# Value and HGRN-gate columns of w_in by seven half-size products (Strassen), with the gate's silu kept in DRAM

## The chip, the cores and the metric

One NeuronCore of a Trainium2 chip runs the whole kernel. Its engines work side by side, each through its own list of instructions in order: TensorE (PE: matmuls, with its weight loads PEld), VectorE (DVE), ScalarE (ACT), GpSimd (POOL) and SyncE (SP), which here mostly issues DMAs. They wait for one another by semaphores. The metric is the device time of one execution in microseconds; three runs were taken, and one more with the profiler.

## The reference, cut to what matters

```python
u = rmsnorm(h, g_pre)                  # 1024 tokens x 2048, float32
z = u @ w_in                           # w_in: 2048 x 9216
aq, ak, av, ag, hq, hf_f, hf_b, hv, hg = jnp.split(z, SPLIT_IDX, axis=-1)   # 1024 columns each
...
o_fw = hgrn2_direction(qh, vh, heads(hf_f, HG_HEADS), lb_f)    # scan over the tokens, 8 heads of 128
...
o_hg = rmsnorm(o_fw + o_bw, g_hg).reshape(B, S, HG_W)
y_hg = o_hg * jax.nn.silu(hg.astype(f32))
y = jnp.concatenate([y_att, y_hg], axis=-1) @ w_out
```

The columns of `w_in` that matter here are av (2048 to 3071), hv (7168 to 8191) and hg (8192 to 9215). Behind this follow the output product, two normalizations and a gated embedding product, which the change doesn't touch.

## The kernel before

float32 products are made of three matmuls each: both operands are split into a rounded high part and a residual, and high x high, high x residual and residual (bfloat16) x high are added up in one PSUM bank. `K.uh` holds the high part of the normalized activations u, transposed (two halves of 512 tokens, 16 tiles of 128 rows of K each), `K.ul` their residual in bfloat16. A weight piece (`piece`, line 71) is loaded into `raw` (three buffers), rounded by ScalarE (`wh`, line 82), its residual taken by GpSimd, now and then by VectorE (`wl`, line 83), and cast to bfloat16 by VectorE (`wb`, line 84). `wh`, `wl` and `wb` have three buffers each.

The program has these stages. First x is normalized in eight tiles of 128 tokens (`prenorm`): ScalarE squares, VectorE scales (line 167), TensorE transposes (line 171), ScalarE and VectorE split the result into `uh` (line 150) and `ul` (line 151). Beside it and after it `v_group` makes the 2048 value columns in four groups of 512, with a bank for each 128 tokens and 16 steps of K; a step has 24 matmuls for 8 banks. The group's first two quarters of the tokens stand between the tiles of the normalization. The results go to `vD` in DRAM.

Then comes the HGRN loop, eight heads (`hgrn`). A head has four column groups of 128 columns (`group`, 96 matmuls of 512 columns each): forget gate forward and backward (into `F2`), query (`hq`), and gate (`hgt`, by `gate_evac`, which multiplies with the sigmoid). Between them stands the scan: a ladder of seven levels in which VectorE multiplies prefix products (line 281, tiles `X`, `O`, `Q2`, `TB`), with small matmuls on each level (`pl`, `pa`, lines 275, 300 and 307); then transposes (`ptr`), state products (`pu`, line 366) with a chain of VectorE additions (`hst`, line 372), output products (`pout`, lines 385 to 389), the normalization over a head (`hsq`, `hss`, `hon`, line 398), and, after the next head's first group (`flush`, `finish`), transposes (`po`) and the product with `hgt` (`hyt`, line 407). After that come eight attention units and the output stages.

PSUM has eight banks: four of the name `gb` for column groups, four for all else (`wk`: `xp`, `vb`, `pl`, `pa`, `ptr`, `pu`, `pout`, `po`). A scheduler that knows the program order, buffers and priorities sets each engine's list; weight pieces of the groups are given a higher priority, so they are fetched early. Inside the list of an engine nothing overtakes.

Of the kernel before, what the change touches and what calls it, by code (L numbers as in the profile page):

```python
# [21 lines left out]
S = 1024  # L22
D = 2048
INW = 9216
KT = 16
# [3 lines left out]
NGB = 4  # L29
# [7 lines left out]
def f32(t):  # L37
    return t.bitcast(F32)
# [6 lines left out]
class Kern:  # L45
    def __init__(self, tc, ctx):
        self.tc = tc
        self.nc = tc.nc
        self.ctx = ctx
        nc = self.nc  # L50
        self.cp = ctx.enter_context(tc.tile_pool(name="cp", bufs=1))
        self.wp = ctx.enter_context(tc.tile_pool(name="wp", bufs=3))
        self.ps = ctx.enter_context(tc.tile_pool(name="ps", bufs=1, space=PSUM))
        self.dr = ctx.enter_context(tc.tile_pool(name="dr", bufs=1, space=DRAM))
        self.ident = self.cp.tile([128, 128], F32, name="ident")
        make_identity(nc, self.ident)
        self.rest = None
# [170 lines left out]
    def hgrn(self, w_in, h, vsrc, yout):  # L228
        nc = self.nc
        V = nc.vector  # L230
# [13 lines left out]
        base = 4096 + 128 * h  # L244
# [3 lines left out]
        q = big.tile([128, S], F32, name="hq", tag="hq", bufs=1)  # L248
# [7 lines left out]
        TB = big.tile([128, 2032], F32, name="TB", tag="ht", bufs=1)  # L256
# [9 lines left out]
        n = S  # L266
# [15 lines left out]
        while B < 128:  # L282
# [29 lines left out]
            x = X[:, :]  # L312
# [23 lines left out]
            n = nb  # L336
# [22 lines left out]
        for d in range(2):  # L359
# [3 lines left out]
            for g in (order[:4], order[4:]):  # L363
                p = self.wk("pu", (128, 4, 128))
# [341 lines left out]
def tile_hybrid(ctx, tc, x, p, positions, w_in, w_out, g_pre, g_post, g_hg, lb_fwd, lb_bwd, w_pg, w_pp, g_ple, out):  # L706
    nc = tc.nc
    K = Kern(tc, ctx)
    x2 = x[0]
    out2 = out[0]  # L710
    w_in = w_in[0]
# [14 lines left out]
    V = nc.vector  # L726
    vD = [K.dr.tile([S, 512], F32, name=f"vD{i}") for i in range(4)]

    def v_group(cg, toks, pool):
        c0 = (2048, 2560, 7168, 7680)[cg]  # L730
        pb = {t: (K.gb() if t < NGB else K.wk("vb")) for t in toks}
        for k in range(KT):
            wh, wl, wb = K.piece(w_in[128 * k:128 * k + 128, c0:c0 + 512], [512], prio=False,
                                 sub=V if len(toks) == 2 and k % 2 else None)
            for t in toks:
                hi = K.uh[t // 4][:, k, 128 * (t % 4):128 * (t % 4) + 128]
                nc.tensor.matmul(pb[t], hi, wh, start=(k == 0), stop=False)  # L737
                nc.tensor.matmul(pb[t], hi, wl, start=False, stop=False)  # L738
            for t in toks:
                lo = K.ul[t // 4][:, k, 128 * (t % 4):128 * (t % 4) + 128]  # L740
                nc.tensor.matmul(pb[t], lo, wb, start=False, stop=(k == KT - 1))
        for t in toks:
            vo = pool.tile([128, 512], F32, name="vo", tag="vo", bufs=3)
            (nc.scalar.copy if t % 2 else V.tensor_copy)(vo, pb[t])
            nc.sync.dma_start(vD[cg][128 * t:128 * t + 128, :], vo)

    with tc.tile_pool(name="p0", bufs=1) as p0:
        warm = K.sp.tile([128, 1], F32, name="warm", bufs=1)
        V.memset(warm, 1.0)
        nc.scalar.activation(warm, warm, AF.Sqrt)  # L750
        K.prenorm(x2, g_pre, p0, (0, 1))
        v_group(0, (0, 1), p0)
        K.prenorm(x2, g_pre, p0, (2, 3))
        v_group(0, (2, 3), p0)
        late = K.prenorm(x2, g_pre, p0, (4, 5, 6, 7))
        v_group(0, (4, 5, 6, 7), p0)
        with tc.issue_after(late[0].ins), tc.issue_after(late[1].ins):
            K.hg_consts((lb_fwd, lb_bwd), g_hg)
# [269 lines left out]
```

## Time and profile before

| | us |
|---|---|
| median of three runs (2910.19 to 2912.11) | 2910.5 |
| the profiled execution | 2911.69 |
| its span, first to last instruction | 2909.9 |
| TensorE busy | 2785.7 |
| VectorE busy | 1508.4 |
| GpSimd busy | 1023.8 |
| ScalarE busy | 925.5 |

The mean granted TensorE clock was 0.992 of full speed. A row of a group gives line, engine, operation, output <- inputs, shape and count, then the busy time and the mean duration of one. A row of the timeline gives start and duration in us, then the same names; in brackets stands how long the engine had been idle and what ended that. Busy times of matmuls overlap, so the pace of matmuls is read from their starts, not from their durations.

### The profile page before, as it was taken

To read this page: it belongs to the slowest core of one execution; us is meant where nothing else is said; L and a number is where in the kernel's file an instruction comes from. 1 tells how busy PE (TensorE), PEld (TensorE's weight loads), DVE (VectorE), ACT (ScalarE), POOL (GpSimd) and SP (SyncE) were. 2 spreads that over 40 slices of the span, in tenths; PEclk is the share of its full clock that TensorE was granted. 3 is DMA by queue.
4 is the path that set the end of the run, shared out by engine and by line. 5 is a ranking of instruction groups with operands and counts; after the bars stand their busy time and mean duration, and the time that the engine had idled before them with its cause. 6 is when DMAs were issued, how large, how long until landed. Compare 5 with 4: busy or idle time off the path is not lost. (4 is left out here: it accounts for less than half of the span.)

```text
span 2909.9 us, 46582 instructions
## 1 busy us (share of the span) xinstructions
PE 2785.7 (96%) x18128; PEld 1885.7 (65%) x18384; DVE 1508.4 (52%) x2833; ACT 925.5 (32%) x1672; POOL 1023.8 (35%) x769
## 2 busy tenths in 40 slices
PE   6999999999999999999999999999999899999997
PEld 4666666676667676676666666666566566665664
DVE  8601116856346346356655555555755645555555
ACT  5311112222122112124434444443533223333323
POOL 2422223413313313322222222222244554666555
PEclk9999999999999999999999999999999999999998
DMA  6412221211111111121221222122344543433453
GB/s 226 121 55 80 77 86 39 66 52 39 57 52 44 52 52 45 51 65 55 78 70 45 73 76 71 47 74 71 113 122 133 159 142 97 131 113 109 146 155 106
DMA packets 251614, 250.54 MB, mean 86 GB/s; under 512 B 21633, under 2 KB 175233, under 8 KB 250241
## 3 DMA queue, kind: packets, MB, share of 16 engines
q1 hardware_dynamic: 242224, 238.62, 27.6%
q10 hardware_dynamic: 9168, 8.93, 0.9%
q8 instruction: 144, 2.36, 0.3%
q14 instruction: 78, 0.63, 0.1%
HBM read 205.54 MB, written 29.36 MB: 81 GB/s over the span
## 5 line engine op out<-in xcount | busy, mean ns | idle before, releaser
L83 POOL TENSOR_TENSOR wl<-raw,wh 128x512 fp32r<-128x512 f32 x568 | 764.7, 1350 | 1599.8 <-ACT wh L82 1507.1
L84 DVE CAST wb<-raw 128x512 bf16<-128x512 f32 x584 | 430.5, 740 | 785.2 <-PE gb L106 281.8
L82 ACT CAST wh<-raw 128x512 fp32r<-128x512 f32 x584 | 358.4, 617 | 1241.7 <-PE gb L101 414.7
L101 PE MATMUL gb<-uh,wh 128*128 128x512 f32 x1792 | 744.3, 415 | 0.0
L102 PE MATMUL gb<-uh,wl 128*128 128x512 f32 x1792 | 708.6, 395 | 0.0
L106 PE MATMUL gb<-ul,wb 128*128 128x512 bf16 x1632 | 405.7, 380 | 9.8 <-issue 1.8
L101 PEld LDWEIGHTS gb<-uh,wh 128*128 128x128 f32 x1792 | 337.1, 188 | 82.9 <-issue 1.2
L102 PEld LDWEIGHTS gb<-uh,wl 128*128 128x128 f32 x1792 | 337.1, 188 | 68.9 <-issue 1.0
L106 PEld LDWEIGHTS <-wb 128*128 128x128 bf16 x1792 | 158.4, 98 | 204.6 <-issue 54.3
L810 PE MATMUL gb<-wh,yh 128*128 128x512 f32 x512 | 231.2, 452 | 2.8 <-DVE Y L842 2.8
L810 PE MATMUL gb<-wh,th 128*128 128x512 f32 x480 | 215.8, 450 | 0.0
L811 PE MATMUL gb<-wl,yh 128*128 128x512 f32 x512 | 203.7, 398 | 4.7 <-POOL wl L83 4.7
L811 PE MATMUL gb<-wl,th 128*128 128x512 f32 x480 | 190.6, 397 | 5.4 <-POOL wl L83 5.4
L645 DVE CUSTOM_DVE_ANT_1 asm<-asc,amask 128x512 f32<-128x512 f32 x128 | 88.3, 690 | 119.9 <-PE asc L639 119.7
L814 PE MATMUL gb<-wb,yl 128*128 128x512 bf16 x479 | 133.7, 383 | 1.6
L814 PE MATMUL gb<-wb,tl 128*128 128x512 bf16 x452 | 126.2, 384 | 1.0
L650 ACT ACTIVATE asm<-asm,anm 128x512 f32<-128x512 f32 x128 | 92.5, 722 | 90.3 <-DVE anm L648 90.0
L810 PEld LDWEIGHTS gb<-wh,yh 128*128 128x128 f32 x512 | 97.6, 191 | 33.3 <-DVE Y L842 3.3
L737 PE MATMUL gb<-wh,uh 128*128 128x512 f32 x256 | 116.4, 461 | 1.4 <-ACT wh L82 1.3
L811 PEld LDWEIGHTS gb<-wl,yh 128*128 128x128 f32 x512 | 97.4, 190 | 24.3 <-POOL wl L83 5.9
L738 PE MATMUL gb<-wl,uh 128*128 128x512 f32 x256 | 102.4, 407 | 10.9 <-POOL wl L83 7.9
L634 PE MATMUL asc<-ak,aqt 128*32 128x256 bf16 x1536 | 109.7, 401 | 3.2 <-issue 2.4
(274 smaller groups left out, 3668.4 us busy)
## 6 DMA issues: line engine op xcount, KB each, us to landing
raw<-in_w_in_dram SPq DMA_DIRECT2D x320, 256.0 KB
raw<-in_w_out_dram SPq DMA_DIRECT2D x128, 256.0 KB
raw<-in_w_pg_dram SPq DMA_DIRECT2D x128, 256.0 KB
xt<-in_x_dram SPq DMA_DIRECT2D x8, 1024.0 KB
vD<-vo SPq DMA_DIRECT2D x32, 256.0 KB
raw<-yD SPq DMA_DIRECT2D x32, 256.0 KB
xr<-in_x_dram SPq DMA_DIRECT2D x32, 256.0 KB
ak<-ak SPq DMA_DIRECT2D x96, 64.0 KB
```

The costliest lines, as they stand in the source:

```text
L82: nc.scalar.copy(wh, raw)
L83: (sub or nc.gpsimd).tensor_tensor(wl, raw, f32(wh), op=ALU.subtract)
L84: nc.vector.tensor_copy(wb, raw)
L101: nc.tensor.matmul(pb[hf], wh[:, k], self.uh[hf][:, kt], start=(kt == 0), stop=False)
L102: nc.tensor.matmul(pb[hf], wl[:, k], self.uh[hf][:, kt], start=False, stop=False)
L106: mm = nc.tensor.matmul(pb[hf], wb[:, k], self.ul[hf][:, kt], start=False, stop=(kt == KT - 1))
L634: t = nc.tensor.matmul(sc[32 * r:32 * r + 32, :256], qb[:, sq, 32 * r:32 * r + 32], KS[s][:, h, r::4], start=(s == 0), stop=False, skip_gr ...
L737: nc.tensor.matmul(pb[t], hi, wh, start=(k == 0), stop=False)
L738: nc.tensor.matmul(pb[t], hi, wl, start=False, stop=False)
L810: nc.tensor.matmul(pb[t], a, pc[0], start=first, stop=False)
L811: nc.tensor.matmul(pb[t], a, pc[1], start=False, stop=False)
L814: nc.tensor.matmul(pb[t], lo[:, k, 128 * t:128 * t + 128], pc[2], start=False, stop=last)
```

## The change

The value columns (av and hv) and the gate columns (hg) are computed in three blocks of 1024 columns. Each block is a 2 x 2 division of tokens (512 each), K (1024 each) and columns (512 each), and in place of eight half-size products it makes seven, in Winograd's form of Strassen's algorithm: "11", "21", "T2", "T1", "T3", "22" and "T4", each with 8 steps of K and 12 matmuls a step on four banks. Four of them ("T2", "T1", "T3", "22") use sums of the activations. `s_build` makes these four sums once, on VectorE, GpSimd and ScalarE, splits them and writes them to DRAM (`sD`); the blocks read them back through a ring of three buffers (`rh`, `rl`). The weights' differences are made for each block in `weights`, from two or three loaded pieces; `TB` keeps one difference for reuse. Partial results are copied out of PSUM (`copies`) and added. The gate block's results go through sigmoid and product (`z_out`) to `zD` in DRAM, transposed as the loop wants them; the loop loads a head's 128 rows in place of computing the gate group. The normalization is interleaved with product "11" of the first block alone.

```diff
         gt = big.tile([128, S], F32, name="hgt", tag="gt", bufs=1)
-        self.group(w_in, base + 4096, lambda hf, p: self.gate_evac(gt[:, 512 * hf:512 * hf + 512], p))
+        nc.sync.dma_start(gt, self.zD["hg"][h])
...
-    def v_group(cg, toks, pool):
...
+    def s_build(pool, kk):
+        def x(name):
+            return pool.tile([128, 512], F32, name=name, tag=name, bufs=2)
+
+        (a11, l11), (a12, l12), (a21, l21), (a22, l22) = [
+            (f32(K.uh[r][:, kk + 8 * c]), K.ul[r][:, kk + 8 * c]) for r in range(2) for c in range(2)]
+        x0, x1, x2 = x("sx0"), x("sx1"), x("sx2")
+        add(x1, a21, l21, nc.gpsimd)
+        add(x2, a22, l22, nc.gpsimd)
+        add(x0, a11, l11)
+        add(x2, x1, x2)
+        s2 = x("sx3")
+        sub(s2, x2, x0)
+        sub(x1, x0, x1)
+        sub(x0, a12, s2)
+        add(x0, x0, l12)
+        for i, t in enumerate((x2, s2, x1, x0)):
+            h = pool.tile([128, 512], F32R, name="sxh", tag="sxh", bufs=3)
+            l = pool.tile([128, 512], BF16, name="sxl", tag="sxl", bufs=3)
+            nc.scalar.copy(h, t)
+            sub(l, t, f32(h), nc.gpsimd if i == 3 else V)
+            nc.sync.dma_start(sD[i][0][:, kk], f32(h))
+            nc.sync.dma_start(sD[i][1][:, kk], l)
...
+        def raw(self, kk, r, c, second=False):
+            if second:
+                t = ring_pool[0].tile([128, 512], F32, name="rb", tag="rb", bufs=4)
+            else:
+                t = K.wp.tile([128, 512], F32, name="raw", tag="raw", bufs=3)
+            k = kk + 8 * r
+            nc.sync.dma_start(t, w_in[128 * k:128 * k + 128, self.cols[c]:self.cols[c] + 512])
+            return t
...
+            elif name == "T2":
+                t = self.raw(kk, 0, 1)
+                sub(t, t, self.raw(kk, 0, 0, True))
+                d = self.TB[:, kk]
+                sub(d, self.raw(kk, 1, 1, True), t)
+                t = d
+            elif name == "T1":
+                t = self.raw(kk, 1, 1)
+                sub(t, t, self.TB[:, kk])
+            elif name == "T3":
+                t = self.raw(kk, 1, 1)
+                sub(t, t, self.raw(kk, 0, 1, True))
+            else:
+                t = self.raw(kk, 1, 0)
+                sub(t, t, self.TB[:, kk])
...
+            nc.scalar.copy(wh, t)
+            sub(wl, t, f32(wh), nc.gpsimd)
+            V.tensor_copy(wb, t)
...
+            c1 = self.copies(0, "tA")
+            self.open(1)
+            self.product(1, orig(0, 1), "21", True)
+            for c in range(4):
+                add(c1[c], c1[c], self.pb[1][c])
+                self.out(0, 0, c, c1[c])
+            self.TB = ring_pool[0].tile([128, 8, 512], F32, name="TB", tag="TB", bufs=1)
+            self.ring = ring_pool[0]
+            self.product(0, comb(1), "T2", False)
+            u = self.copies(0, "tB")
+            self.open(1)
+            self.product(1, comb(0), "T1", True)
+            p5 = self.copies(1, "tA")
+            self.product(0, comb(2), "T3", False)
+            for c in range(4):
+                add(p5[c], p5[c], self.pb[0][c])
+                self.out(1, 1, c, p5[c])
+            self.product(1, comb(3), "22", False)
+            for c in range(4):
+                add(u[c], u[c], self.pb[1][c])
+                self.out(0, 1, c, u[c])
+            self.product(0, orig(1, 1), "T4", False)
...
+            sg = pool.tile([128, 512], F32, name="zsg", tag="zsg", bufs=2)
+            nc.scalar.activation(sg, t, AF.Sigmoid)
+            nc.gpsimd.tensor_tensor(t, t, sg, op=ALU.mult)
+            nc.sync.dma_start(zD[name][4 * n + c][:, 512 * r:512 * r + 512], t)
...
-        v_group(0, (0, 1), p0)
...
-        for cg in range(1, 4):
-            v_group(cg, tuple(range(8)), p0)
+        b0 = Block((2048, 2560), False, v_out(0), p0, False)
...
+        with tc.tile_pool(name="p0s", bufs=1) as p0s:
+            for kk in range(8):
+                s_build(p0s, kk)
+        with tc.tile_pool(name="p0r", bufs=1) as p0r:
+            ring_pool[0] = p0r
+            b0.run(lambda b: None)
...
+            Block((7168, 7680), False, v_out(2), p0, True).run()
+            Block((8192, 8704), True, z_out("hg", p0), p0, False).run()
```

The line numbers in the pieces that follow are those of the changed kernel: 735 and 738 are the adds and subtractions, 809 the cast `wb`, 761 and 762 the stores of the sums, 779 a weight load, 852 and 853 the loads of the sums, 894 the store of a value tile.

VectorE's list, in the middle of the making of the sums (`sx`: the sums, `sxh` and `sxl` their two parts; `wb_1101` is a piece of product "21"):

```order
L738 TENSOR_TENSOR sxl_810<-sx1_786,sxh_809 128x512
L735 TENSOR_TENSOR sx2_823<-sx1_822,sx2_823 128x512
L809 CAST wb_1101<-raw_1097 128x512
L738 TENSOR_TENSOR sx3_828<-sx2_823,sx0_821 128x512
L738 TENSOR_TENSOR sx1_822<-sx0_821,sx1_822 128x512
L738 TENSOR_TENSOR sxl_834<-sx2_823,sxh_833 128x512
L738 TENSOR_TENSOR sx0_821<-uh0_94,sx3_828 128x512
L738 TENSOR_TENSOR sxl_840<-sx3_828,sxh_839 128x512
L735 TENSOR_TENSOR sx0_821<-sx0_821,ul0_96 128x512
L738 TENSOR_TENSOR sxl_846<-sx1_822,sxh_845 128x512
```

Before, constants and casts of `v_group`'s pieces stood at this place; now 72 such adds stand there, with the casts of product "21" among them, the last cast behind the last add.

SyncE's queue, from the end of the sums to the first loads of product "T2" of the first block (`tA`: the tiles c1):

```order
L761 DMA sh3_108<-sxh_995 128x512
L762 DMA sl3_109<-sxl_996 128x512
L894 DMA vD0_98<-tA_1005 128x512
L894 DMA vD0_98<-tA_1006 128x512
L894 DMA vD0_98<-tA_1007 128x512
L894 DMA vD0_98<-tA_1008 128x512
L852 DMA rh_1186<-sh1_104 128x2048
L853 DMA rl_1187<-sl1_105 128x2048
L779 DMA rb_1192<-in_w_in_dram 128x512
L779 DMA rb_1195<-in_w_in_dram 128x512
```

The loads for "T2" stand behind four stores of results of the products "11" and "21".

TensorE's list in a head of the loop, from the second state products on. Before:

```order
L366 MATMUL pu_3730<-hvt_2955,hk1_3699 128x128 x4
L366 MATMUL pu_3739<-hvt_2955,hk1_3699 128x128 x3
L106 LDWEIGHTS wb_3817
L106 MATMUL gb_3747<-ul0_96,wb_3817 128x512
L106 LDWEIGHTS wb_3817
L106 MATMUL gb_3748<-ul1_97,wb_3817 128x512
```

Now, in the same place of a head:

```order
L366 MATMUL pu_7523<-hvt_6732,hk1_7492 128x128 x4
L366 MATMUL pu_7532<-hvt_6732,hk1_7492 128x128 x3
L385 MATMUL pout_7542<-hvt_6732,ATT_7472 128x128
L106 LDWEIGHTS wb_7665
L106 MATMUL gb_7595<-ul0_96,wb_7665 128x512
L106 LDWEIGHTS wb_7665
L106 MATMUL gb_7595<-ul0_96,wb_7665 128x512
```

`gb_3747` and `gb_3748` are the head's own gate group, `gb_7595` and `gb_7596` the next head's first group (forget gate forward). Before, 29 matmuls of the group follow here, and the products `pout` after them; now 7 follow, then the other `pout`, then 22 matmuls of the group, and then the transposes `po`. In the ladder ahead of this place the next head's group takes the positions of the gate group: 67 matmuls between the same small products.

More of the change, by code (lines that the diff above doesn't have):

```diff
@@ L727, in tile_hybrid @@
     vD = [K.dr.tile([S, 512], F32, name=f"vD{i}") for i in range(4)]
-    def v_group(cg, toks, pool):
[L730 to L745, printed above, removed]
+    sD = [(K.dr.tile([128, 8, 512], F32, name=f"sh{i}"), K.dr.tile([128, 8, 512], BF16, name=f"sl{i}")) for i in range(4)]
@@ new lines, in tile_hybrid, with add, sub @@
+    zD = {n: [K.dr.tile([128, S], F32, name=f"z{n}{i}") for i in range(8)] for n in ("hg",)}
+    def add(out, a, b, eng=None):
+        (eng or V).tensor_tensor(out, a, b, op=ALU.add)
+    def sub(out, a, b, eng=None):
+        (eng or V).tensor_tensor(out, a, b, op=ALU.subtract)
+    def s_build(pool, kk):
[20 more added lines that the diff above has]
+            nc.sync.dma_start(sD[i][1][:, kk], l)
@@ L750, in tile_hybrid, with start @@
         nc.scalar.activation(warm, warm, AF.Sqrt)
-        K.prenorm(x2, g_pre, p0, (0, 1))
-        v_group(0, (0, 1), p0)
[L753 to L758, printed above, removed]
-        for cg in range(1, 4):
-            v_group(cg, tuple(range(8)), p0)
+        b0 = Block((2048, 2560), False, v_out(0), p0, False)
+        late = None
+        with tc.tile_pool(name="p0a", bufs=1) as p0a:
+            def start(b):
+                b.open(0)
+                act = lambda kk: (K.uh[0][:, kk], K.ul[0][:, kk])
+                K.prenorm(x2, g_pre, p0a, (0, 1))
+                b.product(0, act, "11", True, (0, 1))
+                K.prenorm(x2, g_pre, p0a, (2, 3))
+                b.product(0, act, "11", True, (2, 3))
+                return K.prenorm(x2, g_pre, p0a, (4, 5, 6, 7))
+            late = start(b0)
+        with tc.tile_pool(name="p0s", bufs=1) as p0s:
+            for kk in range(8):
+                s_build(p0s, kk)
+        with tc.tile_pool(name="p0r", bufs=1) as p0r:
+            ring_pool[0] = p0r
+            b0.run(lambda b: None)
+            with tc.issue_after(late[0].ins), tc.issue_after(late[1].ins):
+                K.hg_consts((lb_fwd, lb_bwd), g_hg)
+            Block((7168, 7680), False, v_out(2), p0, True).run()
+            Block((8192, 8704), True, z_out("hg", p0), p0, False).run()
+    K.zD = zD
     with tc.tile_pool(name="big", bufs=1) as big:
```

72 lines of the change are left out of this document (added).

## The prediction

> **What bounds the kernel now.** The page's table of busy time comes first, then its strip of 40 slices.
>
> ```profile
> span 2909.9 us, 46582 instructions
> PE 2785.7 (96%) x18128; PEld 1885.7 (65%) x18384; DVE 1508.4 (52%) x2833; ACT 925.5 (32%) x1672; POOL 1023.8 (35%) x769
> PE   6999999999999999999999999999999899999997
> DVE  8601116856346346356655555555755645555555
> ```
>
> TensorE is busy from the second slice to the last, so the kernel is as long as its matmuls, with a weak place only in the first 73 us. So I price matmuls first, and then ask where VectorE (DVE), GpSimd (POOL) or a DMA must finish before TensorE can go on. The stages by the table of windows, and the ends of the stages by the views of lines and sources:
>
> ```profile
> 0.00:100.30 100.30, 71.41 (x322) 46.02 (x328) 80.53 (x142) 55.95 (x95) 33.12 (x28) 0.97 0.60 202
> 100.30:401.40 301.10, 300.21 (x1315) 204.95 (x1337) 51.08 (x134) 47.36 (x78) 80.98 (x64) 1.00 0.26 74
> 655.00:764.10 109.10, 105.26 (x954) 75.60 (x964) 54.52 (x107) 22.34 (x37) 31.94 (x25) 1.00 0.17 49
> 873.00:982.00 109.00, 105.22 (x954) 75.83 (x964) 53.88 (x108) 22.33 (x37) 31.88 (x25) 1.00 0.17 50
> L101 PE MATMUL gb<-uh,wh x1792: 387/389/586, 401.4 to 2047.2; 128*128 128x512 f32 x200
> L407 DVE SCALAR_TENSOR_TENSOR hyt<-po,ghg,hgt x16: 736/740/746, 546.2 to 1309.9; 128x512 f32<-128x512 f32 x16
> ```
>
> The columns after a window's length are PE, weight loads, DVE, ACT, POOL, clock, DMA share and GB/s. The normalization of x ends near 100.3 us and is VectorE's (80.53 of 100.30); the value columns fill 301 us with TensorE idle for 1; the HGRN loop starts at 401.4. A head takes 109 us ((1309.9 - 546.2)/7), of which TensorE is busy for 105 and VectorE for 54.
>
> **What a matmul costs.** Durations overlap, so I take the pace, from the stage that already has 12 matmuls to each weight piece:
>
> ```profile
> 115.58 0.43 DVE L84 CAST wb<-raw 128x512 bf16<-128x512 f32 x1 [1.07 <-DMA raw<-in_w_in_dram]
> 118.01 1.21 DVE L84 CAST wb<-raw 128x512 bf16<-128x512 f32 x1 [2.00 <-PE vb L741]
> 120.73 1.21 DVE L84 CAST wb<-raw 128x512 bf16<-128x512 f32 x1 [1.52 <-PE vb L741]
> 120.36 1.29 POOL L83 TENSOR_TENSOR wl<-raw,wh 128x512 fp32r<-128x512 f32 x1 [1.43 <-ACT wh L82]
> 119.67 0.62 ACT L82 CAST wh<-raw 128x512 fp32r<-128x512 f32 x1 [2.11 <-PE vb L737]
> ```
>
> A piece every 2.72 to 2.73 us for 12 matmuls is 0.2273 us each. Before, four value groups of 384 and eight gates of 96 make 2304 matmuls; now three blocks of 7 products x 8 steps x 12 make 2016. **288 fewer are worth 65.5 us.** A product step lasts 2.73 us, and everything else has to fit into that.
>
> **Start.** Prenorm stays, with half as many weight pieces beside it. VectorE's groups in the first 100.3 us:
>
> ```profile
> L84 DVE CAST wb<-raw 128x512 bf16<-128x512 f32 x35 | 24.0, 706 | 5.4 <-DMA raw<-in_w_in_dram 2.6 <-PE gb L741 1.6 <-PE gb L738 1.2
> L83 DVE TENSOR_TENSOR wl<-raw,wh 128x512 fp32r<-128x512 f32 x16 | 14.2, 889 | 3.1 <-ACT wh L82 3.1
> L744 DVE COPY vo<-gb 128x512 f32<-128x512 f32 x2 | 1.4, 685 | 0.0
> ```
>
> The 16 subtractions, 18 of 35 casts (12.7 us) and the copies go: 80.5 - 14.2 - 12.7 - 1.4 = 52 us, and with the same 20 us of gaps the normalization ends at 72 (62 to 80). By then 96 matmuls are done; before, 194 were by 100.3 (322 records less 128 transposes). The x loads are as they were.
>
> **Building the activation sums** (s_build, 8 steps). VectorE has 9 two-input adds a step, GpSimd 3, ScalarE 4 copies, and all read SBUF. What two such engines do to each other is shown in the HGRN ladder:
>
> ```profile
> 689.44 0.69 DVE L281 TENSOR_TENSOR Q<-Q,F 128x512 f32<-128x512 f32 x1
> 689.54 1.73 POOL L83 TENSOR_TENSOR wl<-raw,wh 128x512 fp32r<-128x512 f32 x1 [6.38 <-ACT wh L82]
> 690.04 1.78 DVE L281 TENSOR_TENSOR X<-X,TB 128x512 f32<-128x512 f32 x1
> 694.29 0.68 DVE L281 TENSOR_TENSOR X<-X,TB 128x512 f32<-128x512 f32 x1
> ```
>
> Alone the VectorE add takes 0.68, and the GpSimd one 1.27 (the row at 96.16, below). Here GpSimd, begun at 689.54, ends at 691.27, about 1.2 us after VectorE lets go, and VectorE's next add ends 0.55 after that. They take turns. So a step costs 9 x 0.55 + 3 x 1.27 = 8.8 us, eight 70; the five weight pieces of product 21 that stand among them add 5 x (1.27 + 0.43) = 8.5, and some waiting makes **80 us**. Bounds: 46 if VectorE's 72 adds, back to back at 0.61 (6.14 for ten in the row at 94.14, below), and 5 casts were all; 95 if the three-deep buffers for the sums' parts add 15. Hidden inside: ScalarE's 32 copies x 0.62 = 20 us, 64 stores x 0.33 = 21 us of SP's queue, and their 12.6 MB, some 42 us at the rate worked out next. The Trainium skill (SBUF — State Buffer, section "SBUF: two separate sides") has the two share an exclusive port pair, held for the whole instruction, when the VectorE operation has two SBUF inputs. The rows agree that one blocks the other; with whole durations (9 x 0.68) the sum by that rule would be 88 us.
>
> Of these 80 us TensorE can use 22: the order has only product 21 there, its last cast behind the last add of the sums. So **58 us of idle TensorE** are new. Nothing covers them: T2 needs the sums, and no later product is ahead of it.
>
> **From product 21 to T2.** SP's queue has the four c1 stores ahead of T2's loads, and these stores wait for VectorE's adds after product 21. Rows for the rate of weight loads, and for a DMA issue (min/median/max in ns):
>
> ```profile
> 112.00:116.00 4.00, 4.00 (x18) 2.78 (x18) 2.86 (x7) 1.07 (x2) 1.30 (x1) 1.00 0.48 138
> 40.00:60.00 20.00, 15.70 (x72) 9.49 (x74) 19.97 (x40) 11.01 (x22) 8.20 (x5) 1.00 0.50 158
> 0.00:20.00 20.00, 6.59 (x23) 4.80 (x23) 10.38 (x22) 12.12 (x18) 3.95 (x11) 1.00 0.79 314
> L745 SPq DMA_DIRECT2D vD<-vo x32: 319/326/561, 59.4 to 408.6; - x32
> ```
>
> 138/0.48 and 158/0.50 give about 300 GB/s for full DMA engines with rows of 2 KB, 314/0.79 nearly 400 with long rows. First add and issue 1 us (the last stores of the sums, whose space T2's buffers take over, end about then), then 1 MB of stores, 1.5 MB of sums and 0.5 MB of weights: 3.1 MB at 300 are 10.5 us, and two subtractions, the rounding and the residual 3 more: **14 us** (8 to 20). The 60 small constant operations on VectorE lie in this gap. TensorE then starts slowly, as it did at the beginning:
>
> ```profile
> 18.54 0.99 PE L737 MATMUL gb<-wh,uh 128*128 128x512 f32 x1
> 19.84 0.99 PE L737 MATMUL gb<-wh,uh 128*128 128x512 f32 x1
> ```
>
> Three matmuls in 1.30 us are 0.43 each, half the pace, for some 5 us: 2 us lost. The Trainium skill (TensorE: Matmul & The Clock Gate, section "What's actually happening") says that the array runs at half clock after about 3.4 us idle and until it was busy for as long; by that rule 1.7 us are lost here, and the rule speaks against every product whose steps leave such gaps.
>
> **The products.** A step has 2.73 us. Turns at the shared access: 1.27 (wl) and 0.43 (cast) always, 0.55 to 0.68 for each weight subtraction: 2.3 to 2.4 for T1, T3 and T4, which fits, and 2.8 to 3.1 for T2. In T2 VectorE has also four c1 adds with a PSUM input, 0.61 each by ten of that kind, which a GpSimd operation among them neither slows nor is slowed by:
>
> ```profile
> 94.14 6.14 DVE L151 TENSOR_TENSOR ul<-xp,uh 128x512 bf16<-128x512 f32 x10 [0.57 <-ACT uh L150]
> 96.16 1.27 POOL L83 TENSOR_TENSOR wl<-raw,wh 128x512 fp32r<-128x512 f32 x1 [1.68 <-PE xp L171]
> ```
>
> T2 loads three weight pieces a step, 0.79 MB or 2.6 us, and sums besides, of which the later blocks have three buffers loaded ahead. T2 thus takes 24 (8 x 3.0) to 27 us (with the four adds behind a blocked one) for 21.8: I take 3 and 4 over, and 8 in the gate block, where four GpSimd products for silu (4 x 1.27 = 5 us) fall into T2 too: **15 us** in all (0 to 40). The other products I cost at nothing, copies and stores included: by the first rows ScalarE is busy 0.62, GpSimd 1.29 and VectorE 1.21 of 2.73, and TensorE did not wait. Without that cover each step would show its residual, 1.3 us.
>
> The loop then starts at 72 + 80 + 1 + 14 + 2 + 15 + 1824 x 0.2273 (415) = 599 instead of 401.4: **197 us later**.
>
> **The HGRN loop.** Eight gate groups of 96 x 0.2273 = 21.8 us go: 174.6. They did not only cost: they were TensorE's filler while VectorE climbs the ladder. The order now has the next head's first group in the same 67 places, so the ladder stays covered. What gets thin is behind it:
>
> ```profile
> 712.58 1.83 PE L366 MATMUL pu<-hvt,hk 128*128 128x128 f32 x14 [1.12 <-DVE hk L352]
> 715.87 1.49 DVE L372 SCALAR_TENSOR_TENSOR hst<-hst,TB,pu 128x128 f32<-128x128 f32 x4
> 725.42 0.39 PE L387 MATMUL pout<-hst,Q 128*128 128x128 f32 x2
> 729.71 1.29 DVE L398 TENSOR_TENSOR hon<-pout,hr 128x512 f32<-128x512 f32 x2
> ```
>
> Between the second pu and pout stood 29 matmuls, now 7: TensorE arrives at 716 with the state chain ending at 717.4, 1.3 us. From pout to po2 the order has 22 matmuls, 5.0 us, for a chain of 5.2 (725.8 to 731.0): 0.2. With some tenths for handing over I take 2 us a head (0 to 4), 16 in all, so the loop gains **158.6**. The gate's load (512 KB a head at a DMA share of 0.17) costs nothing. The attention and all behind it stand in the same order.
>
> **Sum.** +197 - 158.6 = +38.6 us, worked out in a span of 2909.9. That profiled execution took 2911.69 (1.8 lie around the span), the median of the runs is 2910.5; I add to the median: **2949 us**.
>
> **Rivals.**
> 1. *The two engines don't take turns* (in the sums above all). Then the sums take 46 us (-34), T2 loses 3 in place of 15 (-12), and the 17 casts beside the normalization take 0.43 and not 0.71 (-5): 2949 - 51 = 2898, a gain. It decides when the sums take under some 45 us. For it: the change has no dependence between most of these adds, and GpSimd has only 37 us of them; against: the rows at 689. 0.27, of which half faster and half within the bound, since some turn-taking will stay.
> 2. *DMA bounds T2 and T3.* If T2's 1.18 MB a step (weights and sums) come at 300 GB/s without a lead, a step takes 3.9 us, 1.2 too long, and T3's 0.92 MB 3.1, 0.35 too long: 24 x 1.55 = 37 us in place of 15; with it a T2 start of 20 us: 2977. For it: one queue, buffers three or four deep, stores among the loads; against: loads stand ahead in the order. 0.13.
> 3. *The ladder loses its filler.* If the next head's group can't run there, 67 x 0.2273 = 15 us a head come back: 2949 + 122 = 3071. Against: the same PSUM banks are free, and the tile its result goes to is last read on the ladder's first level. 0.03.
>
> The forecast, slower by 10 to 65 us, has 0.57. A measurement can tell some 0.2% (5.8 us) from no change. So faster 0.14 and the same 0.13 (both from rival 1), slower 0.73. The range, 2896 to 2985, holds the forecast, rival 2 for the most part and rival 1 but for its low end; left out are some 0.15, with rival 3. The forecast's own range is 2920 to 2975.
>
> **What would show it.** Right: TensorE mostly idle from about 72 to 165 us, with VectorE and GpSimd busy there and their durations well over 0.68 and 1.27; the loop's first matmul near 600; a head every 89 us. Wrong: sums done within 50 us, T2 steps over 3.5 us, or heads over 93.

## The result, and the profile after

| | before | changed |
|---|---|---|
| median, us | 2910.35 (2907.28 to 2912.11, 4 runs) | 2957.18 (2953.34 to 2960.72, 4 runs) |
| span of the profiled execution, us | 2909.9 | 2951.9 |
| TensorE busy, us | 2785.7 | 2744.3 |
| first matmul of the loop, us | 401.4 | 607.6 |

The ratio is 1.0162 (95% interval 1.0142 to 1.0181): slower, by 47 us. First the page of the changed kernel, with the busy table and the strips of 40 slices (a slice is 74 us; the digit is the busy share in tenths, under PEclk the granted TensorE clock):

```profile
span 2951.9 us, 47249 instructions
PE 2744.3 (93%) x17839; PEld 1842.0 (62%) x18096; DVE 1738.4 (59%) x3067; ACT 987.1 (33%) x1778; POOL 1184.0 (40%) x873
PE   6479999999899999999999999999999999999997
PEclk9689999999999999999999999999999999999998
```

TensorE has 41 us less to do and the span is 42 us longer: 83 us more of it are idle. The idle time stands in the second and third slice, where the clock is low as well. The table of windows of the changed kernel shows that place, and behind it the first two T2 products (166 to 196 and 329.5 to 351.2) and a window of the loop (columns after the length: PE, weight loads, DVE, ACT, POOL, clock, DMA share, GB/s):

```profile
60.00:100.00 40.00, 25.96 (x114) 16.90 (x114) 38.24 (x43) 17.24 (x30) 25.80 (x17) 0.84 0.37 105
100.00:120.00 20.00, 4.56 (x11) 2.99 (x12) 19.51 (x22) 5.55 (x10) 11.15 (x8) 0.59 0.50 175
120.00:140.00 20.00, 4.26 (x12) 2.57 (x12) 18.84 (x23) 6.66 (x11) 10.49 (x7) 0.59 0.57 193
140.00:160.00 20.00, 6.78 (x16) 3.54 (x15) 16.41 (x75) 4.81 (x8) 6.78 (x2) 0.59 0.73 258
166.00:196.00 30.00, 25.51 (x95) 15.48 (x98) 19.68 (x27) 7.16 (x13) 11.46 (x9) 0.91 0.88 313
...
329.50:351.20 21.70, 21.65 (x96) 14.55 (x97) 17.50 (x22) 4.33 (x7) 11.91 (x8) 1.00 0.89 306
...
827.20:915.30 88.10, 84.58 (x861) 61.66 (x871) 51.32 (x101) 18.68 (x31) 26.16 (x20) 1.00 0.19 56
```

From 100 to 160 us TensorE is busy for 16 of 60, VectorE for 55: the stage belongs to the sums. TensorE's waits up to 170 us and the matmuls of product 21 in it (rounded weights by the part of u) say the same:

```profile
PE vb L823 <- DVE wb L809: 46.9, 5, 13.5
```

```profile
L823 PE MATMUL vb<-wh,uh x32: 387/579/988, 74.3 to 147.2; 128*128 128x512 f32 x32
```

Product 21, worth 21.8 us, begins at 74.3 and ends past 150, since its casts (wb) stand among VectorE's additions. How long one addition takes there is read from the groups, by form, from 72 to 152 us (first three rows VectorE, then GpSimd; busy time, mean ns of one, idle time before with what ended it):

```profile
L738 DVE TENSOR_TENSOR sxl<-sx,sxh 128x512 bf16<-128x512 f32 x24 | 25.5, 1061 | 3.2 <-issue 3.2
L735 DVE TENSOR_TENSOR sx<-sx,sx 128x512 f32<-128x512 f32 x8 | 10.3, 1292 | 1.1 <-POOL sx L735 1.1
L735 DVE TENSOR_TENSOR sx<-uh,ul 128x512 f32<-128x512 f32 x8 | 7.2, 900 | 2.3 <-POOL sxl L738 2.3
...
L738 POOL TENSOR_TENSOR sxl<-sx,sxh 128x512 bf16<-128x512 f32 x8 | 16.2, 2029 | 8.5 <-DMA sh<-sxh 5.2 <-ACT sxh L759 3.4
```

An addition takes VectorE 0.68 us alone; the groups shown take 0.90 to 1.29 on average where GpSimd works beside them. GpSimd's subtraction takes 2.03 in place of 1.27, and this mean holds one of 5.5; the middle of the eight is 1.58. The end of the sums and the start of T2, from TensorE's timeline (in brackets its idle time and what ended it):

```profile
150.87 1.78 PE L823 MATMUL vb<-wb,ul 128*128 128x512 bf16 x4 [2.85 <-DVE wb L809]
166.03 0.79 PE L823 MATMUL gb<-wh,rh 128*128 128x512 f32 x1 [13.38 <-DMA raw<-in_w_in_dram]
167.44 0.80 PE L823 MATMUL gb<-wl,rh 128*128 128x512 f32 x1 [0.62 <-POOL wl L738]
168.04 0.63 PE L823 MATMUL gb<-wh,rh 128*128 128x512 f32 x1
168.46 0.63 PE L823 MATMUL gb<-wl,rh 128*128 128x512 f32 x1
```

TensorE stands still for 13.4 us, and then a matmul starts every 0.42 us in place of 0.2273.

The loop by its sources, the first matmul of the groups and the last product of each head half:

```profile
L101 PE MATMUL gb<-uh,wh x1536: 387/393/796, 607.6 to 2093.4; 128*128 128x512 f32 x192
L407 DVE SCALAR_TENSOR_TENSOR hyt<-po,ghg,hgt x16: 739/745/748, 739.1 to 1355.8; 128x512 f32<-128x512 f32 x16
```

The loop starts 206.2 us later than before. A head takes (1355.8 - 739.1)/7 = 88.1 us in place of 109.1, and by the last hyt (1355.8 against 1309.9) 45.9 us of the 206.2 are left.

### The profile page after: what moved, and what is told of

Its sections match the earlier page's. It is cut to its first block, busy times and chain, and to the rows that moved or that the text cites. A ratio compares the mean times of both kernels' runs of the same rounds, so it can differ in the third digit from the quotient of the medians.

```text
span 2951.9 us, 47249 instructions
## 1 busy us (share of the span) xinstructions
PE 2744.3 (93%) x17839; PEld 1842.0 (62%) x18096; DVE 1738.4 (59%) x3067; ACT 987.1 (33%) x1778; POOL 1184.0 (40%) x873
## 5 line engine op out<-in xcount | busy, mean ns | idle before, releaser
L83 POOL TENSOR_TENSOR wl<-raw,wh 128x512 fp32r<-128x512 f32 x456 | 615.6, 1354 | 1183.2 <-ACT wh L82 1145.2
L101 PE MATMUL gb<-uh,wh 128*128 128x512 f32 x1536 | 641.9, 418 | 0.2 <-ACT vo L887 0.2
L84 DVE CAST wb<-raw 128x512 bf16<-128x512 f32 x456 | 358.4, 787 | 476.8 <-PE gb L985 208.5
L102 PE MATMUL gb<-uh,wl 128*128 128x512 f32 x1536 | 610.6, 398 | 4.1 <-POOL wl L83 4.1
L82 ACT CAST wh<-raw 128x512 fp32r<-128x512 f32 x456 | 280.2, 616 | 797.2 <-PE gb L101 314.9
L106 PE MATMUL gb<-ul,wb 128*128 128x512 bf16 x1384 | 345.5, 380 | 9.3 <-issue 1.6
L101 PEld LDWEIGHTS gb<-uh,wh 128*128 128x128 f32 x1536 | 290.0, 189 | 71.6 <-issue 1.2
L102 PEld LDWEIGHTS gb<-uh,wl 128*128 128x128 f32 x1536 | 290.0, 189 | 63.4 <-POOL wl L83 4.5
L738 POOL TENSOR_TENSOR wl<-raw,wh 128x512 fp32r<-128x512 f32 x152 | 212.0, 1405 | 215.1 <-ACT wh L807 203.4
L106 PEld LDWEIGHTS <-wb 128*128 128x128 bf16 x1536 | 135.6, 98 | 172.9 <-issue 46.1
L807 ACT CAST wh<-raw 128x512 fp32r<-128x512 f32 x152 | 93.4, 620 | 254.3 <-DVE raw L738 123.1
L809 DVE CAST wb<-raw 128x512 bf16<-128x512 f32 x152 | 122.0, 814 | 73.7 <-DMA raw<-in_w_in_dram 24.0
```

The source lines that it names most:

```text
L82: nc.scalar.copy(wh, raw)
L83: (sub or nc.gpsimd).tensor_tensor(wl, raw, f32(wh), op=ALU.subtract)
L84: nc.vector.tensor_copy(wb, raw)
L101: nc.tensor.matmul(pb[hf], wh[:, k], self.uh[hf][:, kt], start=(kt == 0), stop=False)
L102: nc.tensor.matmul(pb[hf], wl[:, k], self.uh[hf][:, kt], start=False, stop=False)
L106: mm = nc.tensor.matmul(pb[hf], wb[:, k], self.ul[hf][:, kt], start=False, stop=(kt == KT - 1))
```

## The experiments

The theory: TensorE waits for the sums; VectorE and GpSimd block each other in them; the gate block about pays for itself. Rivals: the two engines don't block each other, the stores of the sums are the bound, the queue's order makes the gap ahead of T2, or the Strassen blocks lose their eighth in waits of their own. The runs came in three groups, each beside the kernel before on its chip (medians 2906.62, 2909.25 and 2906.99); times are compared by the ratio to that.

### The sums without GpSimd

```diff
-        add(x1, a21, l21, nc.gpsimd)
-        add(x2, a22, l22, nc.gpsimd)
+        add(x1, a21, l21)
+        add(x2, a22, l22)
...
-            sub(l, t, f32(h), nc.gpsimd if i == 3 else V)
+            sub(l, t, f32(h))
```

> All adds of the sums on VectorE, none on GpSimd. If VectorE and GpSimd take turns at SBUF, the sums take 96 x 0.61 us plus five weight pieces x 1.7 us = 67 us in place of the 77 of the changed kernel (74.5 to 151 us of its trace): about 10 us less, 2947 us. Rival, stores and three-deep buffers bound the sums: no change, 2957. Rival, VectorE's own list bounds them and GpSimd runs beside it: 24 x 0.61 = 15 us more, 2972.

Measured: 2944.08 us, ratio 1.0128 (1.0113 to 1.0144). The residuals of the sums in this run, by tile (min/median/max in ns, first and last start):

```profile
L738 DVE TENSOR_TENSOR sxl<-sx,sxh x32: 676/679/909, 81.9 to 141.8; 128x512 bf16<-128x512 f32 x32
```

VectorE has 96 additions in place of 72, and yet its last starts at 141.8 and not at 149.8: nearly every one takes 0.68 again. A stage that gets shorter when one engine takes over all the work of two shows the blocking. It was not the turns that the prediction thought of, though. GpSimd's timeline in this run:

```profile
70.32 1.27 POOL L738 TENSOR_TENSOR wl<-raw,wh 128x512 fp32r<-128x512 f32 x1 [2.99 <-ACT wh L807]
80.11 59.40 POOL L738 TENSOR_TENSOR wl<-raw,wh 128x512 fp32r<-128x512 f32 x3 [8.51 <-ACT wh L807]
```

Three weight residuals (wl) take 59.4 us, the first of them 56.9. TensorE's wait for it, with product 21 standing still, and the first pause of VectorE after that residual began:

```profile
PE vb L823 <- POOL wl L738: 52.4, 1, 52.4
```

```profile
135.18 0.75 DVE L809 CAST wb<-raw 128x512 bf16<-128x512 f32 x2
141.75 0.91 DVE L738 TENSOR_TENSOR sxl<-sx,sxh 128x512 bf16<-128x512 f32 x1 [5.83 <-DMA sl<-sxl]
```

VectorE works without a pause until 135.93, and the residual ends 1.1 us later (80.11 + 56.94 = 137.05): here GpSimd got no turn until VectorE paused. In the changed kernel that happened once, with the subtraction of 5.5 us (142.25 to 147.71; VectorE's unbroken run ends at 146.57). But GpSimd's other 28 operations from 72 to 152 us got in there, although VectorE's rows show only some 7 us of pauses. What lets GpSimd in at one place and not at the other stays open.

This run gains some 10 us by the ratio, as expected, but only in part where it was expected: the loop starts at 603.0, 4.6 us earlier than in the changed kernel. The rest lies behind the loop, where the traces scatter by as much (see the part on the prediction).

### No sums at all

The sums are left out, and the parts of u are stored in their place, so the products that use them do the same work on other data.

```diff
-        add(x1, a21, l21, nc.gpsimd)
...
+        for i, (r, c) in enumerate(((0, 0), (0, 1), (1, 0), (1, 1))):
+            nc.sync.dma_start(sD[i][0][:, kk], f32(K.uh[r][:, kk + 8 * c]))
+            nc.sync.dma_start(sD[i][1][:, kk], K.ul[r][:, kk + 8 * c])
```

> The adds of the sums, their splitting and all of their work on VectorE, GpSimd and ScalarE are left out; the parts of u themselves are stored in their place, in the same sizes, and read back. If the making of the sums is what TensorE waits for, product 21 runs at its own 22 us and everything behind it moves up by some 55 us: 2902 us. Rival, the 64 stores (12.6 MB, 42 us at 300 GB/s) bound the stage: about 30 us less, 2927. Rival, the loss is spread over the products: no more than 15 us less, 2942 or above.

Measured: 2911.54 us, ratio 1.0015 (1.0004 to 1.0026): between the two. TensorE's longest wait from 60 to 170 us, the loop's first matmul, two rows of SyncE's queue, and a row of TensorE's timeline in this run:

```profile
PE vb L804 <- ACT wh L788: 26.8, 1, 26.8
```

```profile
L101 PE MATMUL gb<-uh,wh x1536: 387/393/796, 565.4 to 2050.1; 128*128 128x512 f32 x192
```

```profile
95.08 0.46 SPq L743 DMA_DIRECT2D sl<-ul  x1
95.63 1.47 SPq L760 DMA_DIRECT2D raw<-in_w_in_dram  x3
```

```profile
124.47 0.58 PE L804 MATMUL gb<-wh,rh 128*128 128x512 f32 x1
```

The loop starts 42.2 us earlier than in the changed kernel, so the additions cost 42 us more than the stores do by themselves. The wait of 26.8 us that is left is the stores': the weight loads of product 21 stand behind the last of them in the queue, and begin at 95.6. The last row is T2's first matmul, 41.6 us earlier than in the changed kernel and with no idle time ahead of it: the gap of 13.4 us between product 21 and T2 went with the additions too, so it is part of the 42.

### The gate back in the loop

The gate block is taken out and the gate group is back in each head.

```diff
-        nc.sync.dma_start(gt, self.zD["hg"][h])
+        self.group(w_in, base + 4096, lambda hf, p: self.gate_evac(gt[:, 512 * hf:512 * hf + 512], p))
...
-            Block((8192, 8704), True, z_out("hg", p0), p0, False).run()
```

> The gate block is taken out and the gate groups are back in the loop; the two value blocks stay. If TensorE is the bound in both places, the stage ahead of the loop loses a block of some 155 us and the loop gets back 8 x 21 = 168: 2957 - 155 + 166 = 2968 us, heads of 109 us. Rival, the gate groups were free filler in the loop: 2957 - 155 = 2802, heads of 88 us.

Measured: 2948.71 us, ratio 1.0145 (1.0127 to 1.0163). The sources of this run:

```profile
L101 PE MATMUL gb<-uh,wh x1792: 387/391/586, 444.8 to 2089.7; 128*128 128x512 f32 x200
L407 DVE SCALAR_TENSOR_TENSOR hyt<-po,ghg,hgt x16: 737/740/745, 589.2 to 1352.4; 128x512 f32<-128x512 f32 x16
```

Neither expectation: the gate block costs 607.6 - 444.8 = 163 us ahead of the loop and saves 159 in it (907.6 from the loop's first matmul to the last hyt here, 748.2 with the block), so it gives nothing. Its 672 matmuls are worth 672 x 0.2273 = 153, so 10 are waits of its own.

### The gate ahead of the loop without Strassen

The kernel before, with the gate's eight plain groups ahead of the loop.

```diff
-        self.group(w_in, base + 4096, lambda hf, p: self.gate_evac(gt[:, 512 * hf:512 * hf + 512], p))
+        nc.sync.dma_start(gt, self.zD[h])
...
+        for h in range(8):
+            K.group(w_in, 8192 + 128 * h, z_sink(h))
```

> The kernel before with the gate's eight products made plainly ahead of the loop and its silu kept in DRAM, as the change keeps it; no Strassen product at all. Theory (moving the gate changes little by itself: a loop head gets about 20 us shorter, eight plain groups cost 8 times 21.8 = 175 us ahead of it): 12 to 16 us above the kernel before, about 2920. Rival (the move pays by itself, the loop gets shorter by all of the 21.8 us per head): within 2 us of the kernel before, about 2907.

Measured: 2917.02 us, ratio 1.0031 (1.0019 to 1.0042): 8 us slower, between the two. The last product of a head in this run:

```profile
L407 DVE SCALAR_TENSOR_TENSOR hyt<-po,ghg,hgt x16: 736/746/748, 705.0 to 1322.1; 128x512 f32<-128x512 f32 x16
```

By the loop's end, at 1322.1 against 1309.9, 12 us are lost with no Strassen product in the kernel. So the move by itself takes back 8 to 12 us of the 21.8 that the block's eighth saves.

### The queue ahead of T2

The four stores of c1 stand behind T2's loads, in each block.

```diff
             for c in range(4):
                 add(c1[c], c1[c], self.pb[1][c])
-                self.out(0, 0, c, c1[c])
...
             self.product(0, comb(1), "T2", False)
+            for c in range(4):
+                self.out(0, 0, c, c1[c])
```

> The changed kernel with the first block's four result stores issued behind the loads of product T2 rather than ahead of them, in each of the two blocks. Theory (the 13.4 us gap between products 21 and T2 is the queue: stores that wait for their additions stand ahead of T2's first loads): the gap falls to about 10 us and the time by 3 to 6 us, about 2948 against 2953 for the changed kernel on this chip. Rival (the gap is the buffers that the sums hold and the three-load chain of T2's first weights): no change, 2952 to 2954.

Measured: 2954.11 us, ratio 1.0151 (1.0138 to 1.0165), which can't be told from the changed kernel's: the rival was right. TensorE's timeline of this run, then SyncE's queue in it (start and duration), and the queue in the changed kernel:

```profile
167.48 0.80 PE L823 MATMUL gb<-wh,rh 128*128 128x512 f32 x1 [13.86 <-ACT wh L807]
```

```profile
153.31 0.32 SPq L762 DMA_DIRECT2D sl<-sxl  x1
...
156.37 2.58 SPq L779 DMA_DIRECT2D rb<-in_w_in_dram  x4
```

```profile
152.42 0.32 SPq L762 DMA_DIRECT2D sl<-sxl  x1
...
156.28 1.10 SPq L779 DMA_DIRECT2D rb<-in_w_in_dram  x2
```

The gap stays at 13.9 us. The loads of rb are issued at 156.4 here and at 156.3 there, 3 to 4 us behind the last store of the sums, with the stores of c1 between or not. So those stores are not the cause. That the ring's buffers take over the space of the sums, and wait for that last store, would fit, and so would the missing gap in the run without the sums, which has no such buffers; but there T2's loads also went out while product 21 still ran. It was not tried by itself.

### The first value block plain, the sums beneath it

The first 1024 value columns are computed as before the change, and the sums, all on VectorE, stand among the steps of the second group of 512. The other two blocks stay.

```diff
-            late = start(b0)
+            v_group(0, (0, 1), p0)
...
-            for kk in range(8):
-                s_build(p0s, kk)
+            v_group(1, tuple(range(8)), p0, lambda k: s_build(p0s, k // 2) if k % 2 == 0 else None)
```

> The first 1024 value columns are computed as in the kernel before, the sums (all on VectorE) are made beneath that work, and only the other two blocks take seven products. If the loss is TensorE's idling for the sums, it is hidden here: 2910 - 2 x 21.8 (two blocks save an eighth of 175 us) + 13 (T2 in two blocks) + 4 (loop) = 2884 us. Rival, the adds disturb the weight pieces beneath which they lie, 100 us of turns against 106 us of matmuls with no slack: 25 us come back, 2909. Rival, Strassen's products themselves are slow: above 2915.

Measured: 2931.81 us, ratio 1.0080 (1.0065 to 1.0095): half of the change's loss is gone, but more was expected; by its number alone the run would fit the last rival (Strassen's products themselves slow). Windows of this run, and TensorE's waits up to 600 us:

```profile
120.00:140.00 20.00, 13.53 (x50) 8.93 (x52) 12.64 (x22) 5.89 (x10) 12.59 (x6) 0.74 0.49 160
...
240.00:260.00 20.00, 14.80 (x59) 9.72 (x59) 4.04 (x7) 3.58 (x6) 3.38 (x3) 0.84 0.34 118
```

```profile
PE vb L740 <- POOL wl L83: 14.9, 2, 9.7
PE vb L843 <- DVE vo L748: 5.1, 1, 5.1
```

Two causes offer themselves. GpSimd's residuals are shut out again (one wait of 9.7 us), and the clock is low around such waits. And at 240 us the first Strassen block waits for PSUM banks whose results leave slowly, through two buffers.

### Residuals on VectorE, more result buffers

Three edits to that version: over the sums the residuals are VectorE's too; the results leave through the eight buffers tA and tB; the two blocks swap their banks.

```diff
-                                 sub=V if len(toks) == 2 and k % 2 else None)
+                                 sub=V if len(toks) != 2 or k % 2 else None)
...
-            vo = pool.tile([128, 512], F32, name="vo", tag="vo", bufs=2)
+            vo = pool.tile([128, 512], F32, name="vo", tag=("tA", "tB")[t % 2], bufs=4)
...
-            Block((7168, 7680), False, v_out(2), p0, True).run()
-            Block((8192, 8704), True, z_out("hg", p0), p0, False).run()
+            Block((7168, 7680), False, v_out(2), p0, False).run()
+            Block((8192, 8704), True, z_out("hg", p0), p0, True).run()
```

> The plain first value block of the run before this one, with three edits: the weight residuals of all pieces that lie over the sums are formed by VectorE and no longer by GpSimd, the plain products' results leave through eight buffers in place of two, and the two Strassen blocks swap their sets of PSUM banks so that each starts on free banks. Theory (GpSimd kept out by VectorE's back-to-back additions, then a cold TensorE clock, and the wait for result buffers cost that run its gain): it lost 51 us ahead of the loop (loop start 583.6, against 401.4 plus 131 of added matmuls); if only the blocks' own 18 us of waits stay, the loop starts near 550 and the time is about 2898 us, 8 below the kernel before on the same chip. Rival (the losses are the Strassen blocks' own): nothing changes, about 2930 us, loop start near 584.

Measured: **2892.62 us, ratio 0.9945 (0.9931 to 0.9959): faster than both kernels**, 17 us below the one before. The windows of this run:

```profile
100.00:120.00 20.00, 19.95 (x90) 13.18 (x89) 18.20 (x58) 8.75 (x15) 0.00 (x0) 1.00 0.60 158
120.00:140.00 20.00, 19.95 (x88) 13.46 (x89) 20.00 (x38) 8.50 (x15) 0.00 (x0) 1.00 0.72 236
140.00:160.00 20.00, 19.29 (x85) 12.90 (x85) 20.00 (x36) 8.10 (x14) 0.00 (x0) 1.00 0.81 276
...
240.00:260.00 20.00, 19.95 (x87) 13.46 (x88) 8.92 (x8) 6.27 (x11) 9.91 (x8) 1.00 0.38 105
```

The same additions now cost TensorE next to nothing: from 100 to 160 us VectorE is busy for 58.2 of 60, GpSimd does nothing, TensorE is busy for 59.2, and the clock is granted in full. The sources of this run:

```profile
L101 PE MATMUL gb<-uh,wh x1536: 387/393/796, 546.2 to 2031.2; 128*128 128x512 f32 x192
L407 DVE SCALAR_TENSOR_TENSOR hyt<-po,ghg,hgt x16: 735/746/748, 677.8 to 1294.0; 128x512 f32<-128x512 f32 x16
```

The loop starts at 546.2 us, 61 earlier than in the changed kernel, though one block is plain again and has 21.8 us of matmuls more.

### The same without the gate block

```diff
-        nc.sync.dma_start(gt, self.zD["hg"][h])
+        self.group(w_in, base + 4096, lambda hf, p: self.gate_evac(gt[:, 512 * hf:512 * hf + 512], p))
...
-            Block((8192, 8704), True, z_out("hg", p0), p0, True).run()
```

> As the run ahead of it, with the gate block taken out and the gate's product back in the loop, so that one Strassen block (the gate columns' neighbours, value columns 7168 to 8191) is all that is left of the change. Theory (the gate block costs about 163 us ahead of the loop and saves about 160 to 164 in it): the time of the run ahead of it within 5 us. Rival (the block saves its eighth, 21.8 us, wherever the sums are hidden): slower than the run ahead by 15 to 20 us. Loop period back at 109.

Measured: 2890.16 us, ratio 0.9931 (0.9919 to 0.9944), which can't be told from the run ahead. Its sources:

```profile
L101 PE MATMUL gb<-uh,wh x1792: 387/390/586, 386.8 to 2031.2; 128*128 128x512 f32 x200
L407 DVE SCALAR_TENSOR_TENSOR hyt<-po,ghg,hgt x16: 735/739/746, 531.2 to 1294.6; 128x512 f32<-128x512 f32 x16
```

The gate block costs 546.2 - 386.8 = 159.4 us here and the last hyt is at 1294.0 with it and 1294.6 without: it gives nothing here either. With the one Strassen block that is left, the last hyt is 15.3 us earlier than in the kernel before (1294.6 against 1309.9), and the time 19 us shorter, for the 21.8 that its missing eighth is worth; the difference of the two lies behind the loop. The plain groups' other edits have no run of their own without a Strassen block, but little to gain: TensorE had 1 us of idle time in 301 in that stage before.

### Which of the three edits

One edit taken back, and one alone:

```diff
-                                 sub=V if len(toks) != 2 or k % 2 else None)
+                                 sub=V if len(toks) == 2 and k % 2 else None)
```

> The faster version (plain first value block, weight residuals over the sums on VectorE, eight result buffers, banks swapped) with one of its three edits taken back: the residuals of the pieces over the sums are on GpSimd again. Theory (GpSimd shut out by VectorE's additions, and the TensorE clock that goes cold in those waits, were the larger part of the 39 us between the two versions): about 2912 us, 18 to 28 above the faster version's 2892.6, with waits for GpSimd's residuals between 100 and 160 us and a granted clock below 0.9 there. Rival (the result buffers and banks were the larger part): within 8 us of 2892.6.

```diff
-                                 sub=V if len(toks) == 2 and k % 2 else None)
+                                 sub=V if len(toks) != 2 or k % 2 else None)
```

> The first version with the plain value block (2931.8 us) with one edit alone: the residuals of the pieces over the sums on VectorE; two result buffers and the old order of banks stay. Theory: about 2911 us, since the waits for buffers and the cold stretch at 240 to 260 us (together some 10 to 15 us) stay, and the residual waits go. Rival (the residuals alone are the cause of nothing, buffers are): above 2925.

Measured: 2920.15 us and 2905.32 us. The four ratios with their intervals:

| | residuals over the sums on GpSimd | on VectorE |
|---|---|---|
| two result buffers, old banks | 1.0080 (1.0065 to 1.0095) | 0.9992 (0.9983 to 1.0001) |
| eight result buffers, banks swapped | 1.0043 (1.0029 to 1.0057) | 0.9945 (0.9931 to 0.9959) |

The place of the residuals is worth 0.0088 to 0.0098 of 2907 us, 26 to 28 us, and buffers with banks 11 to 14; the two add up. So the larger part is GpSimd's starvation, and the rivals fall. For the run with GpSimd's residuals and eight buffers: its longest wait of TensorE, its windows, and the residuals from 100 to 160 us by tile (min/median/max in ns):

```profile
PE vb L740 <- POOL wl L83: 15.6, 2, 9.7
```

```profile
120.00:140.00 20.00, 10.65 (x39) 7.13 (x41) 12.29 (x21) 4.75 (x8) 14.64 (x5) 0.74 0.48 155
140.00:160.00 20.00, 14.08 (x49) 8.99 (x49) 13.75 (x24) 6.95 (x12) 12.32 (x4) 0.83 0.52 172
```

```profile
L83 POOL TENSOR_TENSOR wl<-raw,wh x13: 1267/1318/10797, 104.1 to 158.0; 128x512 fp32r<-128x512 f32 x13
```

Both waits end 1.2 us after VectorE's run of additions pauses (TensorE goes on at 129.35 and 150.76, VectorE stops at 128.17 and 149.59), as in the run with all sums on VectorE. The waits are 15.6 us and the edit is worth 26 to 28. All of it is lost by the end of the plain products: the last of their matmuls start at 255.2 here and at 229.1 with VectorE's residuals. A granted clock of 0.74 and 0.83 around the waits can make up for most of the rest, which was not tried by itself. The 5.1 us for result buffers are gone here; in the run with the residuals alone they are back (one wait of 5.1 us, as in the first plain version), without the 15.

## Why the prediction was right

Slower was forecast, at 2949; it is 2957. Step by step, from the trace of the changed kernel (the steps add up to the 42.0 us between the two profiled spans; the medians are 46.8 apart):

| step | predicted, us | measured, us |
|---|---|---|
| normalization ends | 72 | 74 |
| sums | 80 | 77 (74 to 151) |
| from product 21 to T2 | 14 | 13.4 |
| losses in T2 and the blocks | 15 | about 25 |
| loop starts later by | 197 | 206.2 |
| loop gains | 158.6 | 160.3 |
| behind the loop | 0 | -3.9 |

- **The sums** came out as priced, and the run with all of them on VectorE confirms the blocking. They cost TensorE 55 us (77 less the 22 that product 21 is worth), and with the gap of 13.4 that is more than the 65.5 that the missing matmuls save. What was wrong in the working is that the "turns" are no rule: they fit the ladder's rows and most of the changed kernel's, but with the sums on VectorE GpSimd waited for VectorE's whole chain. Which of the two happens is not explained: at the ladder's rows VectorE doesn't pause between its additions either. The Trainium skill (SBUF — State Buffer, section "SBUF: two separate sides") has the loser block for the whole of the other's instruction. Here it blocked for a whole chain of them, 56.9 us; the measurement decides.
- **The gap ahead of T2** had the right size for a partly wrong reason: its stores on the queue cost nothing, as the run with the stores behind the loads shows, and without the sums there is no gap.
- **The term that was mis-sized** is the losses in T2 and the blocks. From T2's start to the loop are 441.6 us for 415 of matmuls; of the 26.6 some 2 are the slow start. The prediction put 3, 4 and 8 us into the three T2 and nothing into the other products. By the first matmuls of the products it is otherwise: the first T2 takes 29.8 us (166.0 to 195.8) where 25 were said, the second 21.7 (329.5 to 351.2), its bare matmuls, and the gate block's 24.5 (486.6 to 511.1) where 30 were said. Some 16 us lie in products that were priced at nothing, 10 of them in the three T4 (23.7, 23.4 and 28.3 us for 21.8), where TensorE's waits are for GpSimd's residuals and ScalarE's roundings. So that the 15 came as near as it did is in part luck. The gate block as a whole has 10 us of waits, by the run without it.
- **The loop** gained as said, split otherwise: seven heads gain 21.0 us each of 21.8, and the first one only 13.3 (607.6 to 739.1, against 401.4 to 546.2). Of the 2 us a head for a state chain that comes late, 0.8 showed at most.
- **The 3.9 us behind the loop** have no cause in the change that the trace shows. From the last hyt to the span's end it is 1600.0 before, 1596.1 after, and 1591.5 to 1600.0 over all traces of this document, with the same program there: the 3.9 lie within that scatter.
- **Rivals.** Engines that don't block each other: refuted, by the durations above. DMA as the bound: in the first T2 at most. Its window has a DMA share of 0.88 at 313 GB/s, but the second T2 has 0.89 at 306 and loses nothing, so such a share alone does not make the loss; what does in the first T2 is not shown. The loop without filler: refuted, 88.1 us a head.

The seven products save most of what they promise where little waits: one block gives 15 us of 21.8 up to the loop's end, and 19 in the time of the whole run. The change lost this to sums made where TensorE had nothing else to do, and the saving of the gate block to its move out of the loop and its own waits.

## What to carry to other kernels

Work that saves matmuls by additions must have its additions beneath matmuls that don't need them: the same sums cost TensorE 55 us at one place and about one at another, and one block of plain products was a fair price for that place. Where VectorE runs a long chain of additions with two SBUF inputs, take out of GpSimd's list for that stretch whatever TensorE waits for, even if VectorE then has more to do. And a product moved out of a loop can save less there than its matmuls (here 160 of 175 us); here the move and the block's own waits ate the eighth that was saved on it.

## What the runs showed of the hardware

- VectorE and GpSimd do not share fairly. A GpSimd subtraction that takes 1.27 us alone took 56.9 us, and 10.8 in the plain-block version, while VectorE's additions beside it stayed at 0.68. Both ended 1.1 us after VectorE's next pause began. Elsewhere, in the ladder and for most of the changed kernel's sums, GpSimd got in between two additions and VectorE waited for it; what decides is open.
- Two waits of TensorE, 15.6 us together, stood for 26 us by the end of the plain products. The granted clock was 0.74 to 0.83 in the 40 us around them; that it makes up the difference is likely, not tried by itself.
